# Two layers of a hybrid attention trunk in float32: neighbourhood heads scored in pairs, shared output weights, a fourth load buffer

## The chip, the cores and the metric

One core of one Trainium2 chip runs the whole program. The metric is the device time of one execution in microseconds. The kernel before took 1832.28 us (median of three runs, 1830.18 to 1832.47).

## The reference, cut to what matters

There are 256 latent tokens and 256 context tokens of 1024 features, and two layers with the same weights for both groups of tokens. Each layer is a half-step SwiGLU, then a mixing step, then a second half-step SwiGLU; every sub-layer is normalised on both sides and shifted, scaled and gated by a product with `w_ada`.

```python
def swiglu(h, w1, w2):
    a, b = jnp.split(h @ w1, 2, axis=-1)
    return (jax.nn.silu(a) * b) @ w2
...
    a_lat = neighbourhood_attention(aq, ak, av, akc, avc, rpb)      # 4 heads of 64
    b_lat = pool_mix(pin, pool_w, pool_scale)
...
    c_lat = diff_attention(q1, q2, k1 + k1c, k2 + k2c, v + vc, lam) # 4 heads, two softmaxes each
    y_lat = jnp.concatenate([a_lat, b_lat, c_lat], axis=-1) @ w_out
    if not with_ctx_out:      # the last layer
        return y_lat, None
    a_ctx = dense_attention(aqc, akc, avc)
    b_ctx = pool_mix(pinc, pool_w, pool_scale)
    c_ctx = diff_attention(q1c, q2c, k1c, k2c, vc, lam)
    y_ctx = jnp.concatenate([a_ctx, b_ctx, c_ctx], axis=-1) @ w_out
```

Latent queries see 512 keys (256 latent and 256 context), context queries see the 256 context keys. Layer zero gives both groups of tokens, layer one the latent group alone.

## The kernel before, in words

**Products.** Every float32 product is three products of split operands: an operand is held as a high part (rounded to fp32r) and a low part (the rest), and `mm` (L89) is called for high*high, high*low and low*high. One line (L90) thus records nearly all of TensorE's work. Transposes are recorded where they stand (L482, L536, L802).

**Weights.** A `Unit` (L165) is a weight tile of 512 KB. `load` (L177) brings it into one of three raw buffers (L117) over the queue of SyncE; `parts` splits it: ScalarE writes the high part (L186), VectorE the low part (L191), into a slot of `WS` (three slots), `XS` (five) or `MX` (five). `XS` and `MX` lie in the big tile `R`, which in the mixing step holds `MIXH`, `MIXL`, `PT`, `VAL` and `QK` instead. Units that VectorE reads straight from the raw buffer (`w_ada`, in `ada_v`, L448) are not split; each is read by four multiply-adds (L466).

**Order.** The order is written out by a planner. Work is cut into `Step`s (L206) with an assumed duration, steps that it must follow and delays behind them; `schedule` (L217) places main steps (matrix products) and side steps (attention, norms) on one clock, and `run` (L258) goes through the placed steps, issues the next load as soon as a raw buffer was split or read in that order, and the next split when its slot was given up in that order. A unit whose `after` names a mark is split only behind the step with that mark. Loads and splits go in the order of first use: a unit that can't be split holds up the splits behind it. Each engine works through its instructions in order.

**Modulation.** The products with `w_ada` run on VectorE beside the matrix products of three SwiGLU stages (`take`, L1287, deals out 6, 5 and 5 pieces). A piece's half has four steps of multiply-adds, then `red` (L470: four small products on TensorE sum over partitions, ScalarE copies the sums to `ROWB`, L474), then at once `fin` (L476: two transposes on TensorE, L482, for a shift or scale; for a gate, additions on VectorE into `GROW`, L439). A gate's half begins with `gate_rows` (L428), which loads two rows of constants into `GROW` over SyncE's queue.

**Mixing** (`mixing`, L717). Main steps compute queries and keys of six pairs of heads; side steps are the items. An item of a neighbourhood head (`na_attn`, L954) is one head and 128 queries: three products of 64 features (`scores`, L769) into one of two PSUM banks (`BS`), bias, maximum, exponential with its sum, reciprocal, scaling (L793 to L966), then transposes (`transpose_p`, L799) and the product with the values (`pv`). An item of a differential head (`diff_attn`, L1011) is 128 queries and both softmaxes: `scores2` (L779) issues six products in turn from partitions 0 to 63 and 64 to 127 into both banks. Context items are the same with 256 keys.

**Output product.** `wout_rows` (L1049) multiplies the mixed features by `w_out`, feature block by feature block; in layer zero it is called for the latent and then for the context group, and each call makes its own eight units, which go through the three `WS` slots. Then `tok_end` (L512) normalises and adds, and `pre_pair` (L528) transposes for the next SwiGLU.

## Time and profile before

| | |
|---|---|
| median of three runs | 1832.28 us |
| profiled execution, own time | 1824.12 us |
| its span, first to last instruction | 1822.3 us |
| mean granted TensorE clock | 0.987 |
| instructions | 24374 |
| moved from HBM | 257.51 MB |

A stretch A:B below is in microseconds from the span's start. By the trace the stages are: start to 68; first SwiGLU of layer zero to 400; mixing of layer zero from 455 to 660; its second SwiGLU to 1015 or so; layer one's first SwiGLU to 1400; mixing of layer one from 1456 to 1606; last SwiGLU from 1626. The ends of matrix products are modelled in a profile, so that a TensorE that is always "busy" need not be at its peak; the number of products in a stretch says more.

### The profile page before, as it was taken

How to read it: one execution, taken by the hardware profiler on the slowest of the kernel's cores; microseconds unless marked ns; L12 is line 12 of the kernel's file. 1: busy time of each engine (PE TensorE's matmuls, PEld its weight loads, DVE VectorE, ACT ScalarE, POOL GpSimd, SP SyncE). 2: the span in 40 equal slices, each digit the busy share in tenths (PEclk: the TensorE clock that was granted, in tenths of full speed). 3: DMA queues.
4: the chain of work that ended last, by engine and by line, in shares of the span. 5: the costliest groups of instructions: out<-in, count | busy, mean ns of one | idle time of the engine just before them, and what ended most of it. 6: DMA issues, size and time to landing. Idle time of an engine off the chain costs nothing.

```text
span 1822.3 us, 24374 instructions
## 1 busy us (share of the span) xinstructions
PE 1750.3 (96%) x9496; PEld 1452.9 (80%) x9496; DVE 1170.7 (64%) x1889; ACT 714.8 (39%) x1244; POOL 72.8 (4%) x128
## 2 busy tenths in 40 slices
PE   4999999999999999999999999999999999969998
PEld 3788777778977779878878798888887897859997
DVE  4756776667367875757758565666765737865553
ACT  3323222235267763323222442322223526654442
POOL 0000000001000400000000000000000100200000
PEclk8999999999999999999999999999999999979999
DMA  7836555554211152656545334645554431255662
GB/s 230 243 116 192 176 173 157 167 171 125 57 47 47 64 171 71 188 163 182 176 148 176 124 105 127 197 122 183 176 161 156 115 69 58 93 151 187 187 187 76
DMA packets 301187, 260.19 MB, mean 143 GB/s; under 512 B 18064, under 2 KB 246160, under 8 KB 301072
## 3 DMA queue, kind: packets, MB, share of 16 engines
q1 hardware_dynamic: 297216, 257.67, 46.5%
q8 instruction: 74, 1.21, 0.3%
q10 hardware_dynamic: 3856, 0.97, 0.2%
q14 instruction: 41, 0.34, 0.1%
HBM read 257.51 MB, written 1.10 MB: 142 GB/s over the span
## 4 chain that ended last, share of the span: by engine, by line
PE 65%; DMA 14%; DVE 12%; ACT 5%; issue 3%; POOL 1%; SPq 0%; ACTq 0%; DVEq 0%; POOLq 0%
PE bank L90 62%; DMA raw<-in_ffn_w_dram 10%; DVE sx L466 3%; DVE R L191 2%; ACT R L186 2%; DVE w L191 2%; DMA raw<-in_w_ada_dram 2%; ACT w L186 1%; DMA gtb<-in_w_ada_dram 1%; POOL sr L507 1%; PE bank L802 1%; PE bank L536 1%; DMA csrc<-in_c_dram 1%; DVE sx L464 0%; DVE X L524 0%
## 5 line engine op out<-in xcount | busy, mean ns | idle before, releaser
L90 PE MATMUL bank<-HH,R 128*128 128x512 f32 (+1 forms) x2028 | 531.7, 347 | 4.7 <-ACT R L186 2.5
L90 PE MATMUL bank<-HH,w 128*128 128x512 f32 (+1 forms) x1540 | 433.9, 359 | 0.4 <-DVE w L191 0.4
L90 PEld LDWEIGHTS bank<-HH,R 128*128 128x128 f32 x2028 | 356.3, 191 | 59.5 <-issue 7.2
L90 PE MATMUL bank<-R 128*128 128x512 f32 (+3 forms) x1632 | 364.1, 376 | 2.9 <-DVE YB L642 1.1
L90 PE MATMUL bank<-HL,R 128*128 128x512 f32 (+1 forms) x1014 | 349.5, 345 | 0.0
L90 PEld LDWEIGHTS bank<-R 128*128 128x128 f32 (+1 forms) x1632 | 278.5, 188 | 74.0 <-issue 9.7
L191 DVE TENSOR_TENSOR R<-raw,R 128x1024 fp32r<-128x1024 f32 (+1 forms) x177 | 214.7, 1216 | 173.5 <-ACT R L186 170.1
L466 DVE SCALAR_TENSOR_TENSOR sx<-raw,sc,sx 128x512 f32<-128x512 f32 x448 | 310.8, 745 | 21.8 <-DMA raw<-in_w_ada_dram 21.4
L186 ACT CAST R<-raw 128x1024 fp32r<-128x1024 f32 (+1 forms) x177 | 184.3, 1043 | 343.3 <-DMA raw<-in_ffn_w_dram 270.3
L90 PEld LDWEIGHTS bank<-HH,w 128*128 128x128 f32 x1540 | 274.1, 190 | 50.2 <-issue 12.0
L191 DVE TENSOR_TENSOR w<-raw,w 128x1024 fp32r<-128x1024 f32 (+1 forms) x153 | 187.5, 1226 | 161.8 <-ACT w L186 161.5
L90 PE MATMUL bank<-HL,w 128*128 128x512 f32 (+1 forms) x770 | 274.7, 357 | 0.0
L186 ACT CAST w<-raw 128x1024 fp32r<-128x1024 f32 (+1 forms) x153 | 159.9, 1046 | 279.8 <-DMA raw<-in_ffn_w_dram 199.6
L90 PE MATMUL bank<-w,R 128*128 128x512 f32 x960 | 236.0, 396 | 2.6 <-ACT R L1008 1.8
L90 PEld LDWEIGHTS bank<-w,R 128*128 128x128 f32 x960 | 178.1, 189 | 43.4 <-ACT R L1008 2.3
L90 PEld LDWEIGHTS bank<-HL,R 128*128 128x128 f32 x1014 | 193.3, 191 | 22.4 <-DVE HL L541 0.2
L90 PEld LDWEIGHTS bank<-HL,w 128*128 128x128 f32 x770 | 146.5, 190 | 20.6 <-issue 2.3
L591 DVE TENSOR_TENSOR sil<-sil,bank 128x512 f32<-128x512 f32 (+1 forms) x96 | 55.5, 578 | 77.9 <-PE bank L90 77.7
L593 ACT CAST R<-sil 128x512 fp32r<-128x512 f32 (+1 forms) x96 | 51.2, 533 | 135.0 <-DVE sil L591 135.0
L507 POOL TENSOR_TENSOR sr<-sr,eps 128x1 f32<-128x1 f32 x42 | 28.3, 674 | 1463.5 <-DVE sr L506 1444.5
L590 ACT ACTIVATE sil<-bank 128x512 f32<-128x512 f32 (+1 forms) x96 | 48.9, 510 | 90.7 <-PE bank L90 84.4
L360 DVE TENSOR_TENSOR R<-bank,R 128x512 fp32r<-128x512 f32 (+2 forms) x86 | 47.9, 561 | 33.8 <-ACT R L359 33.5
(145 smaller groups left out, 1211.8 us busy)
## 6 DMA issues: line engine op xcount, KB each, us to landing
raw<-in_ffn_w_dram SPq DMA_DIRECT2D x258, 512.0 KB
raw<-in_w_ada_dram SPq DMA_DIRECT2D x130, 512.0 KB
raw<-in_w_in_dram SPq DMA_DIRECT2D x40, 512.0 KB
raw<-in_w_out_dram SPq DMA_DIRECT2D x24, 512.0 KB
gtb<-in_w_ada_dram SPq DMA_DIRECT2D x10, 512.0 KB
gtb<-gate SPq DMA_DIRECT2D x10, 512.0 KB
raw<-in_ffn_w_dram SPq DMA_DIRECT2D x8, 384.0 KB
sx<-in_w_ada_dram SPq DMA_DIRECT2D x4, 512.0 KB
```

Of the source, the lines that this page charges most:

```text
L90: return nc.tensor.matmul(out=o, lhsT=l, rhs=r, start=start, stop=stop)
L186: ins = S.copy(out=self.hi, in_=self.raw)
L191: ins = self.lo_eng.tensor_tensor(out=self.lo, in0=self.raw, in1=self.hi.bitcast(F32), op=ALU.subtract)
L360: V.tensor_tensor(out=lo, in0=src, in1=hi.bitcast(F32), op=ALU.subtract)
L466: V.scalar_tensor_tensor(out=ACC[v], in0=u.raw[:, z, :], scalar=sv, in1=ACC[v], op0=ALU.mult, op1=ALU.add)
L507: G.tensor_tensor(out=a, in0=a, in1=mhalf, op=ALU.pow)
L536: nc.tensor.transpose(out=pt[:, z, t * P : (t + 1) * P], in_=y[:, t, k * P : (k + 1) * P], identity=ident)
L590: S.activation(out=sl[:, cs], in_=oa, func=AF.Silu)
L591: V.tensor_tensor(out=sl[:, cs], in0=sl[:, cs], in1=ob, op=ALU.mult)
L593: tab["hs"] = S.copy(out=uh[:, cs], in_=sl[:, cs])
L802: nc.tensor.transpose(out=b[:, n * P : (n + 1) * P], in_=e[:, n * P : (n + 1) * P], identity=ident)
```

## The change

- There are four raw buffers in place of three; a scratch tile is halved, and the statistics that wrote to it write to another tile. The ninth hidden slot moves to the end of `R`, so that each of the five `XS` slots covers exactly one tile of the mixing step: `PT`, three `VAL`, two `QK`.
- Neighbourhood heads are scored as differential heads were: both heads of a pair and 128 queries in one step, six products in turn into both banks, then both softmaxes, then two transposes as steps of their own.
- For the context group a step holds two heads (or both softmaxes) and all 256 queries: twelve products, each bank holding two blocks of 256 keys; maxima, reciprocals and transposes cover both blocks.
- `w_out` has eight units in each layer, used by both groups in layer zero. The first three go to `WS`, the others to `XS` slots behind marks: the mixing tile there must have had its last reader.
- `fin` is dealt out two side steps later than `red`, and `gate_rows` two steps later than before.

```diff
-    raws = [tile(f"raw{i}", [1024]) for i in range(3)]
+    raws = [tile(f"raw{i}", [1024]) for i in range(4)]
...
-    JUNK = tile("junk", [D], mybir.dt.bfloat16)
+    JUNK = tile("junk", [T], mybir.dt.bfloat16)
...
-    ST = Ring([tile(f"st{i}", [4]) for i in range(8)])
+    ST = Ring([tile(f"st{i}", [8]) for i in range(8)])
...
-    U_HI = [R[:, i * 1024 : i * 1024 + T] for i in range(NU)]
-    U_LO = [R[:, i * 1024 + T : (i + 1) * 1024] for i in range(NU)]
-    XS = [R[:, 9216 + i * 2048 : 9216 + (i + 1) * 2048].rearrange("p (a n) -> p a n", a=2) for i in range(5)]
+
+    U_AT = [i * 1024 for i in range(8)] + [19456]
+    U_HI = [R[:, i : i + T] for i in U_AT]
+    U_LO = [R[:, i + T : i + 1024] for i in U_AT]
+    XS = [R[:, 8192 + i * 2048 : 8192 + (i + 1) * 2048].rearrange("p (a n) -> p a n", a=2) for i in range(5)]
...
-                if j % 3 == 2:
-                    st.append(Step(lambda l=l, j=j, h=h: gate_rows(l, j, h)))
                 for q in range(4):
+                    if q == 2 and j % 3 == 2:
+                        st.append(Step(lambda l=l, j=j, h=h: gate_rows(l, j, h)))
...
+                st[-1].fin = True
...
+        def scores(q, k, g, qts):
+
+
+            o = [BS() for _ in range(2)]
+            nk = T // len(qts)
+            for n, qt in enumerate(qts):
+                q0 = GROUPS[g].start + qt * P
+                for i, (a, b) in enumerate(((0, 0), (1, 0), (0, 1))):
+                    for j in range(2):
+                        rs = slice(HD * j, HD * j + HD)
+
+                        mm(o[j][:, n * nk : (n + 1) * nk], q[rs, a, q0 : q0 + P], k[rs, b, :nk], i == 0 and n == 0, i == 2 and n == len(qts) - 1)
             return o
...
+        def softmax_exp(os_, es, n):
...
+            for j, o in enumerate(os_):
+                V.reduce_max(out=st[:, j * n : (j + 1) * n], in_=o.rearrange("p (a k) -> p a k", a=n), axis=AX.X, negate=True)
+                for a in range(n):
+                    c_, z = slice(a * T // n, (a + 1) * T // n), j * n + a
+                    behind(S.activation(out=es[j][:, c_], in_=o[:, c_], func=AF.Exp, bias=st[:, z : z + 1], accum_out=st[:, 4 + z : 5 + z]), table())
+            V.reciprocal(out=st[:, 0 : 2 * n], in_=st[:, 4 : 4 + 2 * n])
+            return st
+        def transpose_p(e, qts):
...
+            for i, qt in enumerate(qts):
+                for n in range(nk // P):
+                    nc.tensor.transpose(out=bv[:, n, i * P : (i + 1) * P], in_=e[:, i * nk + n * P : i * nk + (n + 1) * P], identity=ident)
+            split_ps(PT[:, 0, : nk // P, qs], PT[:, 1, : nk // P, qs], bv)
...
+        user = {}
+
+        def softmax_step(box, fn, tiles):
+
+            a = Step(fn, dur=1.0, after=[box["ready"]], needs=[user[z] for z in tiles if z in user])
             if items:
-                a.after.append((items[-1][0], (KN['ia'] * heads) * f + 0.3))
-            if len(items) >= ring:
-                a.needs.append(items[-ring][1])
-            b = Step(s2, dur=0.44 * f, after=[(a, KN['ib'] + (KN['ic'] + 0.8 * heads) * f)])
+                a.after.append((items[-1][0], KN["ia"] * 2 + 0.3))
+            return a
+        def turn_step(box, a, fn, tile_, more=0.0):
+
+            b = Step(fn, dur=0.44, after=[(a, KN["ib"] + KN["ic"] + 1.6 + more)])
...
-                def s1(hh_, qt, g=g, nk=nk, es=es):
-                    o = scores(box["q"], box["k"], HD * hh_, qt, g, nk)
+                po = {}
+
+                def s1(qts, tiles, g=g):
+                    os_ = scores(box["q"], box["k"], g, qts)
                     if g == LAT:
-                        ol = o[:, GROUPS[LAT]].rearrange("p (r c) -> p r c", r=ROWS)
-                        V.tensor_tensor(out=ol, in0=ol, in1=biases[hh_][:, 2 - 2 * qt : 2 - 2 * qt + ROWS, :], op=ALU.add)
-                    e, st = softmax_exp(o, nk, E)
-                    S.activation(out=e, in_=e, func=AF.Copy, scale=st[:, 2:3])
-                    es[hh_, qt] = e
-
-                def s2(hh_, qt, nk=nk, es=es):
-                    transpose_p(es[hh_, qt], nk, qt)
+                        for j, o in enumerate(os_):
+                            ol = o[:, GROUPS[LAT]].rearrange("p (r c) -> p r c", r=ROWS)
+                            V.tensor_tensor(out=ol, in0=ol, in1=biases[j][:, 2 - 2 * qts[0] : 2 - 2 * qts[0] + ROWS, :], op=ALU.add)
+                    n_ = len(qts)
+                    es = [E.t[z] for z in tiles]
+                    st = softmax_exp(os_, es, n_)
+                    for z in range(2 * n_):
+                        e = es[z // n_][:, (z % n_) * T // n_ : (z % n_ + 1) * T // n_]
+                        S.activation(out=e, in_=e, func=AF.Copy, scale=st[:, z : z + 1])
...
+                parts = [((0,), (0, 2)), ((1,), (1, 3))] if g == LAT else [((0, 1), (0, 1))]
...
+                def s1(qts, z, g=g):
+                    os_ = scores(box["q"], box["k"], g, qts)
+                    n_ = len(qts)
+                    es = [E.t[z], E.t[3]]
+                    st = softmax_exp(os_, es, n_)
+                    V.tensor_tensor(out=st[:, n_ : 2 * n_], in0=st[:, n_ : 2 * n_], in1=lam[l][:, 3:4].to_broadcast([P, n_]), op=ALU.mult)
+                    for a in range(n_):
+                        e1, e2 = [e[:, a * T // n_ : (a + 1) * T // n_] for e in es]
+                        S.activation(out=e1, in_=e1, func=AF.Copy, scale=st[:, a : a + 1])
+                        V.scalar_tensor_tensor(out=e1, in0=e2, scalar=st[:, n_ + a : n_ + a + 1], in1=e1, op0=ALU.mult, op1=ALU.add)
...
+                for qts in ((0,), (1,)) if g == LAT else ((0, 1),):
+                    z = e1s()
+                    a = softmax_step(box, lambda qts=qts, z=z, f=s1: f(qts, z), (z, 3))
+                    side += [a, turn_step(box, a, lambda z=z, qts=qts: transpose_p(E.t[z], qts), z)]
...
-            us = [Unit(w_out[l, k * P : (k + 1) * P, :], lo=lo_engine(KN['rowc'] if g == CTXG else KN['rowl'])) for k in ks]
...
+        wu = [Unit(w_out[l, k * P : (k + 1) * P, :]) for k in order]
+        ng = len(out_groups)
+        for name, z in (("nav", prods[: 4 * ng]), ("dv0", prods[: 6 * ng]), ("qk0", [it[0] for it in boxes[4]["items"]]),
+                        ("dv1", prods), ("pt", prods + [it[1] for it in items])):
+            side.append(Step(lambda: None, needs=list(z)))
+            side[-1].mark = f"{name}{l}"
+
+        for u, (sl, name) in zip(wu[3:], ((6, "nav"), (4, "dv0"), (7, "qk0"), (5, "dv1"), (3, "pt"))):
+            u.slots, u.after = (sl,), f"{name}{l}"
         for g in out_groups:
-            rows = wout_rows(g, order)
+            rows = wout_rows(g, order, wu)
...
-        o = []
+        o, late = [], []
         for _ in range(n):
-            o += f(*pieces.pop(0))
-        return o
+            for s in f(*pieces.pop(0)):
+                if s.fin:
+                    late = [s, 2]
+                    continue
+                o.append(s)
+                if late:
+                    late[1] -= 1
+                    if not late[1]:
+                        o.append(late[0])
+                        late = []
+        return o + late[:1]
```

## Rows read from the trace of the kernel before

**Rows 1.** The page: busy time, and the chain that ended last by engine

```profile
PE 1750.3 (96%) x9496; PEld 1452.9 (80%) x9496; DVE 1170.7 (64%) x1889; ACT 714.8 (39%) x1244; POOL 72.8 (4%) x128
...
PE 65%; DMA 14%; DVE 12%; ACT 5%; issue 3%; POOL 1%; SPq 0%; ACTq 0%; DVEq 0%; POOLq 0%
```

**Rows 2.** Busy time by stretch: us, engines busy (instructions), granted clock, DMA share, GB/s

```profile
112.00:360.00 248.00, 241.11 (x1090) 190.53 (x1088) 172.88 (x262) 61.79 (x84) 0.00 (x0) 0.99 0.55 170
210.00:260.00 50.00, 47.00 (x208) 37.37 (x212) 36.64 (x58) 14.00 (x18) 0.00 (x0) 0.97 0.58 179
500.00:620.00 120.00, 119.70 (x612) 89.39 (x611) 90.76 (x226) 86.89 (x225) 12.59 (x26) 1.00 0.15 46
620.00:730.00 110.00, 104.80 (x662) 92.01 (x662) 75.63 (x123) 59.55 (x118) 17.55 (x26) 1.00 0.37 115
730.00:914.00 184.00, 181.35 (x823) 145.75 (x821) 124.19 (x179) 54.75 (x71) 0.00 (x0) 0.99 0.58 180
1136.00:1400.00 264.00, 264.00 (x1211) 212.75 (x1210) 175.96 (x262) 76.57 (x98) 0.00 (x0) 1.00 0.53 162
1500.00:1600.00 100.00, 98.93 (x566) 79.66 (x565) 76.73 (x154) 69.66 (x147) 15.17 (x25) 1.00 0.27 84
1600.00:1626.00 26.00, 9.73 (x33) 6.47 (x31) 18.05 (x27) 14.38 (x29) 2.21 (x4) 0.65 0.63 185
```

**Rows 3.** Who waited for whom, TensorE: us in total, times, longest

```profile
PE bank L482 <- ACT rows L474: 5.3, 3, 2.6
...
PE bank L802 <- DVE R L360: 0.2, 1, 0.2
```

**Rows 4.** Timeline 229.9 to 236.5, three rows: start us, us, engine, line; idle before

```profile
234.99 1.04 ACT L186 CAST R<-raw 128x1024 fp32r<-128x1024 f32 x1 [3.82 <-DMA raw<-in_ffn_w_dram]
235.94 0.38 ACT L474 ACTIVATE rows<-bank 128x256 f32<-128x256 f32 x1
...
236.37 0.48 PE L482 MATMUL bank<-cst,rows 128*128 128x128 f32 x1 [2.63 <-ACT rows L474]
```

**Rows 5.** The DMA queue's waits: SP's own

```profile
SPq L432 <- DVE grow L439: 30.5, 8, 9.1
```

**Rows 6.** Timeline, TensorE, single scores of 256 and of 512 keys, and the next row

```profile
510.38 0.61 PE L90 MATMUL bank<-R 64*128 64x256 f32 x3
510.92 0.49 PE L90 MATMUL bank<-HL,w 128*128 128x512 f32 x1
...
515.38 0.96 PE L90 MATMUL bank<-R 64*128 64x512 f32 x3
516.27 0.50 PE L90 MATMUL bank<-HH,w 128*128 128x512 f32 x1
```

**Rows 7.** Timeline, TensorE, paired scores of 256 and of 512 keys, and the next row

```profile
535.03 0.62 PE L90 MATMUL bank<-R 64*128 64x256 f32 x6
535.58 0.74 PE L90 MATMUL bank<-HH,w 128*128 128x512 f32 x2
...
547.11 0.96 PE L90 MATMUL bank<-R 64*128 64x512 f32 x6
548.00 0.50 PE L90 MATMUL bank<-HH,w 128*128 128x512 f32 x1
```

**Rows 8.** Groups by form, 500 to 620 us: busy, mean ns | idle before

```profile
L795 ACT ACTIVATE YB<-bank,st 128x256 f32<-128x256 f32 x20 | 9.5, 475 | 3.7 <-DVE st L793 3.4 <-DVE YB L1025 0.2
...
L795 ACT ACTIVATION_READ_ACCUMULATOR YB<-bank,st 128x1 f32 x43 | 8.5, 198 | 0.0
...
L966 ACT ACTIVATE YB<-YB,st 128x256 f32<-128x256 f32 x8 | 3.9, 503 | 0.6 <-DVE st L796 0.5
```

**Rows 9.** The page: low parts of units, and the output weights' loads

```profile
L191 DVE TENSOR_TENSOR w<-raw,w 128x1024 fp32r<-128x1024 f32 (+1 forms) x153 | 187.5, 1226 | 161.8 <-ACT w L186 161.5
...
raw<-in_w_out_dram SPq DMA_DIRECT2D x24, 512.0 KB
```

**Rows 10.** Timeline, TensorE: a pair whose second bank came late

```profile
1577.90 1.63 PE L90 MATMUL bank<-R 64*128 64x512 f32 x6 [0.31 <-ACT YB L795]
```

More of the change, by code (lines that the diff above doesn't have):

```diff
@@ L210, in __init__ @@
             self.fn, self.units, self.dur, self.after, self.needs = fn, list(units), dur, list(after), list(needs)
-            self.low = low
+            self.low, self.fin = low, False
             self.t = None
@@ L556, in out_end @@
         for hf in range(2):
[L557 removed]
+            S.activation(out=JUNK, in_=o[hf], func=AF.Square, scale=RMS, accum_out=st[:, hf : hf + 1])
             V.tensor_tensor(out=gy[:, hf * T : (hf + 1) * T], in0=o[hf], in1=GTB[:, LAT, hf * T : (hf + 1) * T], op=ALU.mult)
@@ L790, in softmax_exp @@
-        def softmax_exp(o, nk, ring):
-            st = ST()
-            V.reduce_max(out=st[:, 0:1], in_=o, axis=AX.X, negate=True)
-            e = ring()[:, :nk]
-            behind(S.activation(out=e, in_=o, func=AF.Exp, bias=st[:, 0:1], accum_out=st[:, 1:2]), table())
-            V.reciprocal(out=st[:, 2:3], in_=st[:, 1:2])
-            return e, st
-        def transpose_p(e, nk, qt):
-            b = BT()
-            for n in range(nk // P):
-                nc.tensor.transpose(out=b[:, n * P : (n + 1) * P], in_=e[:, n * P : (n + 1) * P], identity=ident)
-            qs = slice(qt * P, (qt + 1) * P)
-            split_ps(PT[:, 0, : nk // P, qs], PT[:, 1, : nk // P, qs], b[:, :nk].rearrange("p (n q) -> p n q", q=P))
+        def scores(q, k, g, qts):
[7 more added lines that the diff above has]
+                        mm(o[j][:, n * nk : (n + 1) * nk], q[rs, a, q0 : q0 + P], k[rs, b, :nk], i == 0 and n == 0, i == 2 and n == len(qts) - 1)
+            return o
@@ L980, in s3 @@
                             split_ps(MIXH[rs, n, GROUPS[g]], MIXL[rs, n, GROUPS[g]], o[rs, z * SEQ : (z + 1) * SEQ])
-                for hh_ in range(2):
-                    for qt in range(2):
-                        st = item(box, lambda hh_=hh_, qt=qt, f=s1: f(hh_, qt), lambda hh_=hh_, qt=qt, f=s2: f(hh_, qt), nk, 1, 4)
-                        if g == LAT:
-                            st[0].after.append((bias_step, 1.5))
-                        side += st
+                parts = [((0,), (0, 2)), ((1,), (1, 3))] if g == LAT else [((0, 1), (0, 1))]
+                sm = []
+                for qts, tiles in parts:
+                    a = softmax_step(box, lambda qts=qts, tiles=tiles, f=s1: f(qts, tiles), tiles)
+                    if g == LAT:
+                        a.after.append((bias_step, 1.5))
+                    if sm:
+                        a.after.append((sm[-1], KN["ia"] * 2 + 0.3))
+                    sm.append(a)
+                    side.append(a)
+                for hh_ in range(2):
+                    for a, (qts, tiles) in zip(sm, parts):
+                        z = tiles[hh_]
+                        side.append(turn_step(box, a, lambda z=z, qts=qts: transpose_p(E.t[z], qts), z, 0.6 * hh_))
                     side.append(product(lambda hh_=hh_, f=s3: f(hh_), nk))
@@ L1036, in s3 @@
                     S.activation(out=RSTD[g], in_=o, func=AF.Square, scale=math.sqrt(D / P))
-                for qt in range(2):
-                    side += item(box, lambda qt=qt, f=s1: f(qt), lambda qt=qt, f=s2: f(qt), nk, 2, 3)
+                for qts in ((0,), (1,)) if g == LAT else ((0, 1),):
+                    z = e1s()
+                    a = softmax_step(box, lambda qts=qts, z=z, f=s1: f(qts, z), (z, 3))
+                    side += [a, turn_step(box, a, lambda z=z, qts=qts: transpose_p(E.t[z], qts), z)]
                 side.append(product(s3, nk))
@@ L1125, in mixing @@
                 at = diff_attn(n - 2, boxes[n])
-                if n == 2:
-                    at[0].needs += [it[1] for it in items[: -2 * len(out_groups)]]
                 side += ss + at
@@ L1185, in x_stat @@
         for t in range(2):
-            S.activation(out=JUNK, in_=xs[g][:, t], func=AF.Square, scale=RMS, accum_out=st[:, t : t + 1])
+            S.activation(out=S2T, in_=xs[g][:, t], func=AF.Square, scale=RMS, accum_out=st[:, t : t + 1])
         if g == LAT:
```

54 lines of the change are left out of this document (14 added, 40 removed).

## The prediction

> **What bounds the kernel now.** I read the page first. TensorE is busy for 96% of the span, and 65% of the chain that ended last is TensorE's; the rest of that chain is DMA (14%) and VectorE (12%) [rows 1]. So most of the time goes only if TensorE gets less to do, and a smaller part if it no longer waits.
>
> The table by stretch comes next, because a busy TensorE can still be slow. Three stretches are SwiGLU bodies with the same kinds of work: split weights and pieces of `w_ada`. In 1136 to 1400 TensorE starts 1211 products in 264 us, 0.2180 us each, with no idle time. In 112 to 360 it starts 1090 in 248 us, 0.2275 us each, and is idle for 6.9 us; in 730 to 914 it starts 823 in 184 us, 0.2236 us each [rows 2]. At the good stretch's pace the two would take 237.6 and 179.4 us. They lose 10.4 and 4.6 us, together 15.0.
>
> TensorE's waits say where. 5.3 us go to three waits of the transposes at L482 for ScalarE's copy at L474 [rows 3]. One of them shows the cause: the copy stands in ScalarE's queue behind the split of a unit whose load has not landed; the split has idled 3.82 us, the copy follows, and TensorE has idled 2.63 us [rows 4]. Around it the granted clock is 0.97 over 50 us: after the idle time a part ran at the lower of its two levels, 1.2 GHz in place of 2.4, and about 1.5 us more were lost [rows 2]. The loads are late because the raw buffers go round: 170 GB/s with three buffers of 0.524 MB means 9.3 us from one load of a buffer to its next [rows 2]. The queue of SyncE also stands still: 30.5 us in eight waits for `GROW` [rows 5].
>
> In mixing TensorE is the bound: it is busy for 119.70 of 120 us in 500 to 620, and for 98.93 of 100 us in 1500 to 1600; the end of layer one's mixing has 16.3 us without products in 1600 to 1626 [rows 2].
>
> **The change part by part.**
>
> *Scores.* A single score of 512 keys keeps TensorE for 0.89 us, from 515.38 to 516.27, and one of 256 keys for 0.54 us [rows 6]. A pair of six products takes the same 0.89 and 0.55 us: the two halves of the array run together [rows 7]. Latent neighbourhood scores: 4 heads, 2 blocks of queries, 2 layers are 16 singles, now 8 pairs; 8 x 0.89 = 7.1 us less. A context step of twelve products is not in the trace. Its bounds are one pair of 512 keys (the same number of columns, 0.89 us) and two pairs of 256 (1.10 us); it is nearest to the first, since nothing stands between its products. Neighbourhood context: 8 x 0.54 - 2 x 0.89 = 2.5 us less (2.1 at the other end). Differential context: 8 x 0.55 - 4 x 0.89 = 0.8 us less (0 at the other end). Together 10.4 us. Against it: a pair needs both banks, and where the second comes late it takes 1.63 instead of 0.96 us as the timeline shows it, 0.67 more [rows 10]. I count three such among 16 latent differential steps; at that rate 14 new steps give 14 x 3/16 x 0.67 = 1.8 us back. I take 8.5 us; the ends are 10.4 and, with every second bank late, 7.1 + 2.1 - 14 x 0.67, which is about nothing.
>
> VectorE and ScalarE do the same bias, maximum, exponential and scaling per key as before, and they cover for TensorE only while there are products between a step and its transposes. In 500 to 620 VectorE is busy for 90.76 us and ScalarE for 86.89 of 120 [rows 2], so a shorter stretch still has room: 112 us would hold both.
>
> Here a page speaks against the change. The Trainium skill, "TensorEngine Tiling (Array Packing)", section "Performance Considerations", says that tiling speeds up TensorE but not the emptying of PSUM, which may then be the bottleneck. By that the term would be nothing and the sum 16 us; by the busy times above it is 8.5 and the sum 24.5.
>
> *Fourth buffer and later `fin`.* At the good stretch's pace the first body needs 170 x 248 / 237.6 = 177 GB/s. Four buffers give 4 x 0.524 MB / 9.3 us = 225 GB/s if the round stays at 9.3 us, and enough up to a round of 11.8. With `fin` two side steps later the transposes find the copy done; queued behind TensorE's wait were all products of the body. `fin` takes its copies, additions and the gate's store with it, on VectorE's and ScalarE's queues, and nothing near needs them: the gates are loaded two thirds through a body. `gate_rows` and its four small loads move behind two weight loads on SyncE; it still waits for `GROW`, right behind the `fin` that reads it, but no longer for TensorE and ScalarE in front of that. If that wait stayed, it would hold up to 9.1 us of loads [rows 5], which is what the fourth buffer covers. The ends are 5.3 us (the transposes' waits alone) and 15.0 us (the good stretch's pace). I take 13, near the upper end, because 1136 to 1400 has the same work; the first loads of a body can still be late.
>
> *Shared output weights.* The 24 loads [rows 9] become 16. Eight splits go, with 8 x 1.23 us of VectorE [rows 9] and about as much of ScalarE (one such copy takes 1.04 us [rows 4]). None of this was TensorE's; what it frees is the wait in 620 to 730, where TensorE idles 5.2 us [rows 2] and the first units of the next SwiGLU queue behind those loads. I take 3 us of the 5.2; the other end is nothing. The new wait: the last two units can be split only behind the last product with the values, and the splits of the next SwiGLU queue behind them. That is 2 x (1.04 + 1.23) = 4.5 us, with three blocks of output rows (12 products each, at 0.22 us some 8 us) as cover. If the cover goes, 4.5 us in each layer are lost.
>
> *Costed at nothing:* the shifted slots (no two live tiles overlap), the halved scratch tile, the first 68 us, the merged maxima and reciprocals off the path, and the chain after the last head in layer one. For these I hold 3 us open in either direction.
>
> **Sum.** 8.5 + 13 + 3 = 24.5 us. The profiled execution took 1824.12 us by its own time and would take 1799.6. The median of the runs is 8.2 us above that execution, so I forecast 1832.28 - 24.5 = 1807.8 us; the forecast's own terms reach from 1800 to 1816.
>
> **The rivals.**
>
> A, *the loads stay late.* The round of a buffer lengthens to 11.8 us as more loads share the engines, and only the transposes' 5.3 us are won: 8.5 + 5.3 + 3 = 16.8, 1815.5 us. For it: the chain in the bodies alternates between loads and VectorE, which is busy for 172.88 of 248 us. Against: the DMA share is only 0.55 there [rows 2].
>
> B, *mixing becomes bound by the softmaxes* (the page's rule above): no gain from scores, 16 us, 1816.3 us. For it: both engines are at three quarters of 500 to 620. Against: TensorE hardly waited for a softmax so far, and its transposes at L802 waited 0.2 us in all [rows 3].
>
> C, *every wait goes*: 10.4 + 15.0 + 5.2 + 3 = 33.6 us, 1798.7 us.
>
> D, *slower: the joint steps end late and TensorE stands at the transposes.* The planner puts transposes 5.6 us behind a step (`turn_step`). A context step has four exponentials of 0.475 + 0.198 and four scalings of 0.503 us on ScalarE alone [rows 8], 4.7 us behind its first maximum. If a split or an evacuation gets in between, TensorE, which takes its queue in order, waits. With 14 joint steps this decides from 24.5 / 14 = 1.75 us each; at 2.5 us each it costs 35 us and the time is 1842.8. Against: differential heads have had two exponentials and the same 5.6 us, at 0.2 us of waits.
>
> E, *the pairs don't run together*: every second bank is late because other users of the two banks shift their turn; 14 x 0.67 = 9.4 us back instead of 1.8, so 16.9 us and 1815.4 us.
>
> **How the numbers follow.** Forecast 0.50, A 0.14, B 0.12, C 0.12, D 0.07, E 0.05. The prediction is the forecast's 1808. The range takes in A, B, C and E with what is held open on either side, and leaves out most of D: 1793 to 1822. Within 0.2% (3.7 us, about what a measurement can tell from no change) nothing but a sum of lower ends remains: 0.03; slower is D without its mild half, 0.05; faster 0.92.
>
> **What would show it.** Right: paired scores of 0.9 us in the neighbourhood part; no waits of L482; the two bodies at 0.219 us or less per product, with a granted clock of 1.00; sixteen loads of `w_out`; less than 3 us without products in 620 to 730's counterpart. Wrong: L802 with microseconds of waits (D, B), bodies still at 0.225 (A), or score steps of 1.5 us (E). A new idle stretch behind the last head of a layer would show the splits without cover.

## The result, and the profile after

The changed kernel takes 1799.97 us (median of 4 runs, 1797.86 to 1804.09) against 1832.12 us of the kernel before beside it (1830.18 to 1832.47): a ratio of 0.9829, 95% interval 0.9808 to 0.9851, or 32 us faster. In a later set on another chip the same two kernels stood at 1802.71 and 1830.46 us, 0.9854 (0.9834 to 0.9873), or 28 us. The forecast was 24.5 us and 1808 us; the range held the time.

The two profiled executions differ by 20.0 us only (1824.12 and 1804.09 us): of each kernel's four executions, the one of before was its fastest, the one of after its slowest. A second profile of each was therefore taken (the experiments `before_again` and `after_again`), and stretches are compared over both.

The page of the changed kernel, busy time by engine and the chain by engine; these answer to [rows 1]:

```profile
PE 1735.8 (96%) x9496; PEld 1447.9 (80%) x9496; DVE 1152.8 (64%) x1815; ACT 704.6 (39%) x1228; POOL 79.3 (4%) x128
...
PE 77%; DMA 8%; DVE 7%; ACT 4%; issue 2%; POOL 1%; ACTq 0%; DVEq 0%; POOLq 0%; SPq 0%
```

TensorE runs the same 9496 instructions in 14.5 us less busy time, and its share of the chain rises from 65 to 77%: DMA falls from 14 to 8% of it, VectorE from 12 to 7%.

Busy time by stretch of the changed kernel, the counterparts of [rows 2]; columns as there:

```profile
112.00:360.00 248.00, 243.92 (x1118) 195.02 (x1117) 181.81 (x274) 66.85 (x88) 0.00 (x0) 0.99 0.60 179
716.00:900.00 184.00, 183.19 (x838) 147.68 (x837) 125.20 (x182) 52.35 (x68) 0.00 (x0) 1.00 0.58 178
500.00:606.00 106.00, 105.15 (x562) 81.01 (x561) 81.76 (x166) 80.23 (x203) 14.66 (x24) 1.00 0.19 59
606.00:716.00 110.00, 106.19 (x676) 94.22 (x676) 66.05 (x112) 53.69 (x114) 16.86 (x26) 1.00 0.27 78
1116.00:1380.00 264.00, 264.00 (x1211) 212.67 (x1210) 172.82 (x259) 74.06 (x96) 0.00 (x0) 1.00 0.52 155
1490.00:1580.00 90.00, 89.35 (x505) 71.00 (x504) 71.83 (x132) 62.81 (x133) 18.45 (x22) 1.00 0.30 93
1580.00:1607.00 27.00, 11.47 (x48) 8.66 (x47) 17.55 (x28) 15.01 (x30) 2.22 (x4) 0.72 0.54 160
```

The second body comes to 184 / 838 = 0.2196 us per product (0.2236 before), the first only to 248 / 1118 = 0.2218 (0.2275 before; the good stretch has 0.2180). The figure of the second body depends on where the stretch is laid: in the second profile of before it is 0.2217 from 730 and 0.2236 from 734 us. Mixing is nearly as full of products as before.

Who waited for whom, the changed kernel: TensorE twice, and SyncE's queue for `GROW`; against [rows 3] and [rows 5]:

```profile
PE bank L538 <- DVE YB L528: 23.3, 8, 7.9
...
PE bank L807 <- DVE YB L1045: 0.8, 3, 0.3
```

```profile
SPq L180 <- DVE grow L440: 27.5, 10, 3.4
```

The waits of the old L482 (now L483) are gone. SyncE still waits 27.5 us for `GROW`, now in front of weight loads, but in steps of 3.4 us at most and not 9.1. Over all rows for `GROW` it waits 36.2 us, before 32.6: the wait was cut into shorter pieces and did not get less. The softmax transposes (L807) wait 1.3 us in all.

The transposes of the modulated activations (L538, `pre_pair`) stand at the start of each stage and serve as milestones. Their groups in the changed kernel: minimum, median and maximum in ns, first and last start in us:

```profile
L538 PE MATMUL bank<-cst,YB x32: 271/273/329, 412.5 to 445.3; 128*128 128x128 f32 x32
...
L538 PE MATMUL bank<-cst,YB x32: 271/273/331, 641.4 to 677.7; 128*128 128x128 f32 x32
...
L538 PE MATMUL bank<-cst,YB x32: 271/273/328, 1026.6 to 1056.9; 128*128 128x128 f32 x32
...
L538 PE MATMUL bank<-cst,YB x32: 271/273/477, 1404.8 to 1440.9; 128*128 128x128 f32 x32
...
L538 PE MATMUL bank<-cst,YB x16: 415/421/476, 1596.5 to 1607.6; 128*128 128x128 f32 x16
```

Differences of these starts give the length of every stage. The same milestones of all kernels run here make the table that the rest rests on (us; "front" is from the first to the last transposes ahead of a mixing, "heads" from there to the first ahead of the next SwiGLU, "w_out 0" from there to the last; a body runs to the next first start):

| kernel | first body | front 0 | heads 0 | w_out 0 | second body | third body | front 1 | heads 1 | to the end |
|---|---|---|---|---|---|---|---|---|---|
| before | 418.1 | 34.7 | 203.1 | 40.1 | 350.1 | 377.8 | 31.8 | 159.9 | 206.7 |
| before_again | 420.8 | 34.9 | 203.1 | 41.3 | 352.0 | 378.5 | 33.1 | 160.4 | 206.7 |
| after | 412.5 | 32.8 | 196.1 | 36.3 | 348.9 | 378.2 | 36.1 | 155.6 | 205.8 |
| after_again | 409.6 | 33.8 | 196.3 | 36.3 | 349.5 | 378.2 | 36.0 | 155.6 | 205.8 |
| p_raw4 | 406.1 | 32.9 | 203.5 | 41.3 | 352.5 | 378.5 | 33.2 | 157.5 | 206.6 |
| p_fin | 417.1 | 35.0 | 203.1 | 41.6 | 347.2 | 381.4 | 32.7 | 160.3 | 206.9 |
| p_pairs | 420.2 | 34.8 | 196.3 | 40.4 | 349.6 | 378.4 | 32.5 | 159.7 | 206.0 |
| p_wout | 417.7 | 34.8 | 202.1 | 36.0 | 350.9 | 378.1 | 31.9 | 157.0 | 206.0 |
| u_fin | 406.5 | 33.0 | 196.0 | 36.4 | 357.6 | 378.4 | 37.2 | 155.4 | 205.8 |
| f_pair | 408.1 | 33.7 | 194.0 | 36.3 | 350.1 | 377.7 | 36.5 | 155.3 | 205.4 |
| f_pair_again | 410.5 | 33.8 | 193.9 | 36.3 | 349.7 | 378.0 | 37.3 | 155.8 | 205.8 |
| f_front | 411.3 | 33.5 | 193.9 | 36.3 | 349.9 | 378.5 | 33.6 | 155.1 | 206.0 |
| f_mix | 406.3 | 33.5 | 193.8 | 36.3 | 349.4 | 378.1 | 33.7 | 157.0 | 205.6 |

The mean of the two profiles of after against that of before: first body -8.4, front 0 -1.5, heads 0 -6.9, w_out 0 -4.4, second body -1.9, third 0, **front 1 +3.6**, heads 1 -4.6, the end -0.9. One stage got longer. Together they make 24.9 us: by the two pairs of profiles the gain is smaller than by the medians.

Two of these boundaries do not part the same work in every kernel. Before, then after, w_out 0 and front 1:

```profile
655.90:696.00 40.10, 36.92 (x232) 32.35 (x232) 33.74 (x51) 26.75 (x51) 4.32 (x6) 1.00 0.58 171
1423.90:1455.70 31.80, 29.23 (x188) 26.09 (x187) 25.15 (x38) 19.09 (x37) 5.22 (x7) 1.00 0.47 130
```

```profile
641.40:677.70 36.30, 33.98 (x207) 29.46 (x208) 28.62 (x46) 21.32 (x44) 4.35 (x6) 1.00 0.41 117
1404.80:1440.90 36.10, 32.78 (x212) 30.05 (x211) 27.77 (x42) 21.25 (x40) 5.51 (x7) 0.97 0.55 134
```

In w_out 0 TensorE starts 25 products fewer, which went to the second body; in front 1 it starts 24 more, which came out of the heads. Sums over both sides of a boundary can be compared: w_out 0 and second body 390.2 and 393.3 us before, 385.2 and 385.8 after; front 1 and heads 1 191.7 and 193.5 before, 191.7 and 191.6 after.

The scores, in TensorE's timeline of the changed kernel: a neighbourhood pair, a differential step that came apart, and the last joint context step, each with the row behind it:

```profile
486.08 0.97 PE L90 MATMUL bank<-R 64*128 64x512 f32 x6
486.98 0.50 PE L90 MATMUL bank<-HH,w 128*128 128x512 f32 x1
...
1538.69 0.96 PE L90 MATMUL bank<-R 64*128 64x512 f32 x3
1539.58 0.38 PE L90 MATMUL bank<-HH,w 128*128 128x256 f32 x1
...
1541.17 0.96 PE L90 MATMUL bank<-R 64*128 64x512 f32 x3
1542.06 0.39 PE L90 MATMUL bank<-HH,w 128*128 128x256 f32 x1
...
607.97 1.19 PE L90 MATMUL bank<-R 64*128 64x256 f32 x12
609.09 0.70 PE L90 MATMUL bank<-sx,YB 128*128 128x256 f32 x2
```

The pair keeps TensorE for 0.90 us, as forecast; the differential step takes twice 0.89 us, because its two heads run one after the other; the twelve products of the context step take 1.12 us. The context steps of differential heads in before, which [rows 7] was to show, ran as two threes as well; one of the eight:

```profile
578.12 0.62 PE L90 MATMUL bank<-R 64*128 64x256 f32 x3
...
580.24 0.61 PE L90 MATMUL bank<-R 64*128 64x256 f32 x3
```

### The profile page after: what moved, and what is told of

The parts are those of the page before. It is cut to its first block, busy times and chain, and to the rows that moved or that the text cites. A ratio compares the mean times of both kernels' runs of the same rounds, so it can differ in the third digit from the quotient of the medians.

```text
span 1802.3 us, 24258 instructions
## 1 busy us (share of the span) xinstructions
PE 1735.8 (96%) x9496; PEld 1447.9 (80%) x9496; DVE 1152.8 (64%) x1815; ACT 704.6 (39%) x1228; POOL 79.3 (4%) x128
## 4 chain that ended last, share of the span: by engine, by line
PE 77%; DMA 8%; DVE 7%; ACT 4%; issue 2%; POOL 1%; ACTq 0%; DVEq 0%; POOLq 0%; SPq 0%
PE bank L90 75%; DMA raw<-in_ffn_w_dram 5%; DVE w L192 1%; DVE R L192 1%; ACT w L187 1%; ACT R L187 1%; DMA gtb<-in_w_ada_dram 1%; PE bank L538 1%; PE bank L807 1%; POOL sr L509 1%; DVE sx L467 1%; DMA raw<-in_w_in_dram 1%; DMA csrc<-in_c_dram 1%; DVE X L526 0%; DVE YB L528 0%
## 5 line engine op out<-in xcount | busy, mean ns | idle before, releaser
L90 PE MATMUL bank<-HH,R 128*128 128x512 f32 (+1 forms) x2012 | 524.7, 346 | 0.0
L90 PEld LDWEIGHTS bank<-HH,R 128*128 128x128 f32 x2012 | 351.8, 189 | 51.9 <-issue 7.2
L90 PE MATMUL bank<-R 128*128 128x512 f32 (+3 forms) x1728 | 381.7, 378 | 5.0 <-ACT YB L642 2.3
L90 PEld LDWEIGHTS bank<-R 128*128 128x128 f32 (+1 forms) x1728 | 293.4, 188 | 75.3 <-issue 6.4
L192 DVE TENSOR_TENSOR R<-raw,R 128x1024 fp32r<-128x1024 f32 (+1 forms) x182 | 220.9, 1219 | 163.9 <-ACT R L187 162.4
L187 ACT CAST R<-raw 128x1024 fp32r<-128x1024 f32 (+1 forms) x182 | 189.3, 1045 | 312.9 <-DMA raw<-in_ffn_w_dram 208.6
L192 DVE TENSOR_TENSOR w<-raw,w 128x1024 fp32r<-128x1024 f32 (+1 forms) x140 | 171.6, 1226 | 157.6 <-ACT w L187 156.4
L187 ACT CAST w<-raw 128x1024 fp32r<-128x1024 f32 (+1 forms) x140 | 146.3, 1046 | 244.4 <-DMA raw<-in_ffn_w_dram 161.4
L90 PE MATMUL bank<-w,R 128*128 128x512 f32 x864 | 209.7, 394 | 3.7 <-DVE YB L644 1.8
L90 PEld LDWEIGHTS bank<-w,R 128*128 128x128 f32 x864 | 159.7, 188 | 42.6 <-issue 3.2
```

Of the source, the lines that this page charges most:

```text
L90: return nc.tensor.matmul(out=o, lhsT=l, rhs=r, start=start, stop=stop)
L187: ins = S.copy(out=self.hi, in_=self.raw)
L192: ins = self.lo_eng.tensor_tensor(out=self.lo, in0=self.raw, in1=self.hi.bitcast(F32), op=ALU.subtract)
```

## The experiments

**The four parts, each alone on the kernel before**, on one chip, against 18 runs of before (median 1830.08 us).

*p_raw4.*

```diff
-    raws = [tile(f"raw{i}", [1024]) for i in range(3)]
+    raws = [tile(f"raw{i}", [1024]) for i in range(4)]
-    JUNK = tile("junk", [D], mybir.dt.bfloat16)
+    JUNK = tile("junk", [T], mybir.dt.bfloat16)
```

> The kernel before with the fourth load buffer alone (and the scratch tile halved to make room). Theory 1, the loads were late because three buffers go round too slowly: both bodies come to 0.219 us per product or less, the three waits of the transposes for the copy of the modulation rows fall below 1 us, and the time falls by 10 to 15 us (ratio 0.992 to 0.9945). Rival, SyncE's queue stands behind the gate rows whatever the number of buffers: the 30 us of SyncE's waits stay, the bodies stay above 0.222 us per product, and no more than 5 us are won (ratio 0.997 to 1.000).

Measured: 1815.05 us, 0.9918 (0.9901 to 0.9934), 15.0 us faster. By stretch, the two bodies, and SyncE's wait:

```profile
112.00:360.00 248.00, 246.56 (x1139) 197.65 (x1137) 186.14 (x282) 70.22 (x91) 0.00 (x0) 1.00 0.60 183
718.00:902.00 184.00, 179.57 (x821) 144.21 (x819) 121.96 (x180) 51.28 (x67) 0.00 (x0) 1.00 0.56 172
```

```profile
SPq L432 <- DVE grow L439: 69.4, 9, 22.8
```

The first body comes to 248 / 1139 = 0.2177 us, better than the good stretch, and ends 12 to 15 us earlier. The second stays at 184 / 821 = 0.2241 us. So theory 1 holds in one body and the rival in the other: SyncE now stands 69.4 us for `GROW`, 36 of them in the first body, where nothing comes late for it, and 29 in the second.

*p_fin.*

```diff
-                if j % 3 == 2:
-                    st.append(Step(lambda l=l, j=j, h=h: gate_rows(l, j, h)))
                 for q in range(4):
+                    if q == 2 and j % 3 == 2:
+                        st.append(Step(lambda l=l, j=j, h=h: gate_rows(l, j, h)))
...
+                if s.fin:
+                    late = [s, 2]
+                    continue
```

> The kernel before with the later closing step of the modulation pieces and the later gate rows alone, three buffers. Theory 1: the transposes' waits (10.9 us in three waits) go, but the loads stay late, so 3 to 6 us are won (ratio 0.997 to 0.998) and the first body stays above 0.222 us per product. Rival a, the waits only move to the next user of a late load: 0 to 2 us (ratio 0.999 to 1.000). Rival b, SyncE's standing queue was the cause of the late loads: 10 us or more (ratio below 0.995) with three buffers only.

Measured: 1826.23 us, 0.9977 (0.9964 to 0.9990), 4 us faster. The two bodies:

```profile
112.00:360.00 248.00, 243.73 (x1114) 192.64 (x1113) 177.46 (x265) 66.09 (x87) 0.00 (x0) 0.99 0.57 172
731.00:915.00 184.00, 182.35 (x833) 146.58 (x832) 125.20 (x183) 53.49 (x69) 0.00 (x0) 1.00 0.58 178
```

As theory 1 has it: 0.2226 us per product in the first body, and 0.2209 in the second, which is where its gain lies (347.2 against 350.1 and 352.0 us). The expectation gave the waits of the transposes as 10.9 us; they are 5.3 in three waits [rows 3], and 4 us came of them. Its third body takes 381.4 us, where every other kernel has 377.7 to 378.5; no run here shows why.

*p_pairs.* The hunks of `scores`, `softmax_exp`, `transpose_p`, `na_attn` and `diff_attn` of the change, on the old slots.

> The kernel before with the paired scores and joint context steps alone. Theory 1: TensorE's time in score steps falls by 8 to 9 us, nearly all in layer 0, and the time with it: 7 to 9 us won (ratio 0.995 to 0.996). Rival a, the end of each mixing is bound by the w_out loads and splits, which come no earlier: 0 to 4 us (ratio 0.998 to 1.000). Rival b, fewer and longer steps also leave the other engines freer: 12 us or more (ratio below 0.9935).

Measured: 1820.61 us, 0.9946 (0.9930 to 0.9963), 9.5 us faster: slightly more than theory 1. The heads of layer zero take 196.3 us in place of 203.1; those of layer one 159.7, as before. TensorE's time in the score steps falls by 6.7 us, less than theory 1 has it, and all of it in layer zero; the other 3 us can be put down to no stage.

*p_wout.* The hunks with `wu`, its marks and the shifted slots.

```diff
-            us = [Unit(w_out[l, k * P : (k + 1) * P, :], lo=lo_engine(...)) for k in ks]
+        wu = [Unit(w_out[l, k * P : (k + 1) * P, :]) for k in order]
+        for u, (sl, name) in zip(wu[3:], ((6, "nav"), (4, "dv0"), (7, "qk0"), (5, "dv1"), (3, "pt"))):
+            u.slots, u.after = (sl,), f"{name}{l}"
```

> The kernel before with the output weights of layer one shared by the two groups alone (and the slots shifted for it). Theory 1: 8 loads and 8 splits fewer free the end of layer zero's mixing: 2 to 5 us (ratio 0.997 to 0.999). Rival a, the last two units can be split only behind the last products, so the gain there is lost again behind the last head: 0 or slower (ratio 1.000 to 1.003). Rival b, the end of the mixing and the start of the next body both gain: over 6 us (ratio below 0.9965).

Measured: 1823.14 us, 0.9959 (0.9943 to 0.9974), 7 us faster; its profiled run was its fastest of seven, 1816.32. More than theory 1, and rival b's figure. By milestones some 3 us lie in the stage of the output weights of layer zero and the body behind it (386.9 together for 390.2; the stage alone falls from 40.1 to 36.0, but with some 25 products fewer), and 3 us where I expected nothing, in front and heads of layer one (188.9 for 191.7), in which the weights serve one group only. There the change gives the units slots of their own too. SyncE's queue, in the timeline of before and then of this kernel, the last six loads of `w_out`:

```profile
1558.72 29.77 SPq L179 DMA_DIRECT2D raw<-in_w_out_dram  x6
```

```profile
1553.26 22.87 SPq L181 DMA_DIRECT2D raw<-in_w_out_dram  x6
```

They go out over 23 us in place of 30. That this is what shortens the stage is likely, but it was not tried by itself; with the fourth buffer alone the stage has 157.5 us too.

The four gains add up to 15.0 + 3.9 + 9.5 + 6.9 = 35.3 us; the changed kernel won 28 to 32. Some 3 to 8 us are lost when the parts meet.

**Second profiles, and two edits of the changed kernel**, on one chip.

> The kernel before, unchanged, for a second profile of it. Its first profiled execution took 1824.1 us by its own time, while its other runs took 1830 to 1832. Theory 1: the runs differ where loads are late, so a profile near 1830 us has the first SwiGLU body (112 to 360 us) and the other weight stretches slower, and the mixing stretches the same to within 1 us. Rival: the runs differ by the granted clock alone, evenly over the span.

Measured: 1832.59 us by the profiled execution. Against the first profile, 8.5 us longer in span: first body +2.7, w_out 0 +1.2, second body +1.9, third +0.7, front 1 +1.3, the rest together +0.7. Theory 1: the stages with many loads differ and heads 0 does not (203.1 both times). That the time of a run of before depends on when its loads land fits this, but is not shown.

> The changed kernel, unchanged, as the measure for the two kernels beside it and for a second profile. Expected: a ratio of 0.981 to 0.985 again, and a profile in which the first body ends earlier than the 412.5 us of the first profile (the first profiled execution was the slowest of its four).

Measured: 1802.71 us, 0.9854 (0.9834 to 0.9873), just outside what I expected; the first body ends at 409.6 us, as expected.

*u_fin*, the p_fin hunks undone in the changed kernel:

> The changed kernel with the closing steps of the modulation pieces and the gate rows back in their old places, four buffers kept. Theory 1, the fourth buffer alone makes the loads punctual, so the old place costs nothing more: within 2 us of the changed kernel run beside it. Rival a, the later place is worth with four buffers what it was worth with three (4.2 us): 3 to 5 us slower than the changed kernel. Rival b, it now holds the work of a later step up: 3 to 6 us faster, with the first body ending near 406 us as with the fourth buffer alone.

Measured: 1808.10 us, 0.9882 (0.9864 to 0.9900), 5.4 us slower than the changed kernel: rival a, and just above its bound. But its stages show two effects. The first body ends 3 us earlier (406.5), as rival b has it; the second takes 8 us more (357.6 for 349.5). TensorE, 690 to 1030 us:

```profile
PE bank L483 <- ACT rows L475: 3.3, 2, 1.8
PE bank L90 <- DVE YB L643: 3.2, 1, 3.2
```

```profile
690.00:1030.00 340.00, 332.00 (x1569) 269.47 (x1568) 214.54 (x314) 97.31 (x137) 2.19 (x4) 0.99 0.52 158
```

The changed kernel, in its second profile, has 338.12 us busy with 1625 products in the same stretch. SyncE stands 29 us for `GROW` there, at most 13.5, as with the fourth buffer alone. So with four buffers the later place is worth 8 us in the second body. That the buffer itself helps there, no run shows: with the old place p_raw4 stands at 352.5 us, no better than before, and u_fin at 357.6 against the 350.9 of p_wout, which has three buffers and the same number of products in that body. `fin` and `gate_rows` went back together, so their shares are not parted.

*f_pair.*

```diff
-                    for j in range(2):
+                    for j in (1, 0):
...
-                        mm(o[j]...)
+                        ins = mm(o[j]...)
+                        if n == 0 and i == 0:
+                            if j == 1:
+                                first = ins
+                            else:
+                                behind(ins, first)
```

> The changed kernel with each score pair kept together: the two heads' first products change places, and the first head's may not be ordered ahead of the second's, so none starts before both banks are free. In the changed kernel about half of the differential steps still run as two separate threes of 0.89 us. Theory 1: TensorE's time in scores falls by another 8 to 14 us, and the time by 5 to 12 us against the changed kernel run beside it. Rival a: the pair now waits for the second bank with nothing else to do, the softmaxes end later, and TensorE's idle time grows by what the pairs save: within 2 us. Rival b: slower by 3 us or more, with waits of the transposes behind the scalings.

Measured: 1798.93 us, 0.9830 (0.9811 to 0.9849), 3.8 us faster than the changed kernel, between theory 1 and rival a. The differential step shown above, in its timeline:

```profile
1535.12 0.97 PE L90 MATMUL bank<-R 64*128 64x512 f32 x6
1536.02 0.50 PE L90 MATMUL bank<-HH,w 128*128 128x256 f32 x2
```

Adding the score steps over the timeline (first product to the next other row): before 29.4 us in layer zero and 15.9 in layer one, after 23.7 and 16.0, here 21.0 and 12.0. The 2.7 us in layer zero shorten its heads by 2.3; the 3.9 us in layer one shorten nothing (155.3 for 155.6): TensorE is busy for 142.1 us of that stage in place of 145.5, so what the pairs save there comes back as idle time, as rival a has it. Two differential steps of layer zero still run as two threes (from 568.29 and from 576.50).

**The longer front of layer one.** In the timeline of `after_again`, SyncE's queue, then ScalarE, then TensorE:

```profile
1416.75 1.34 SPq L824 DMA_DIRECT2D YB<-in_na_rpb_dram  x2
1420.69 0.37 SPq L180 DMA_DIRECT2D raw<-in_w_in_dram  x1
1421.16 2.68 SPq L824 DMA_DIRECT2D YB<-in_na_rpb_dram  x2
...
1427.32 1.05 ACT L187 CAST R<-raw 128x1024 fp32r<-128x1024 f32 x1 [2.72 <-DMA raw<-in_w_in_dram]
1428.28 0.62 ACT L521 ACTIVATE junk<-YB 128x512 bf16<-128x512 f32 x1
...
1435.82 0.44 PE L538 MATMUL bank<-cst,YB 128*128 128x128 f32 x2 [3.17 <-DVE YB L528]
```

The loads of the attention bias go out around a weight load of the front; ScalarE's split idles 2.72 us for its load, the square that the context group's chain needs stands behind it, and TensorE idles 3.17 us for that chain (2.5 us in before). In the issue order of the kernels with the fourth buffer alone, or the shared weights alone, the bias stands behind all of the front's loads; with both parts it passes the last two.

*f_pair_again, f_front, f_mix*, on one chip (before: 1832.03 us).

> The changed kernel with each score pair kept together, unchanged from the run before, as the measure for the two kernels beside it. Expected: a ratio of 0.981 to 0.985 again, and the front of layer one's mixing (from the end of the first SwiGLU to the last modulated transposes) as long as in the changed kernel, 36 us.

Measured: 1802.27 us, 0.9841 (0.9824 to 0.9859); front 1 is 37.3 us. That is 3.3 us above its first set, so its gain over the changed kernel (3.8 us side by side) is about as large as what two sets differ by.

*f_front.*

```diff
         def after_front(ins):
 
-            return behind(ins, early[-1].dma)
+            for u in early:
+                behind(ins, u.dma)
+            return ins
```

> The pairs kept together, and the bias and pooling loads ordered behind all eight weight loads of the mixing's front and not behind the last of them alone. In the changed kernel four to six of these small loads pass the seventh weight load on SyncE's queue; ScalarE's split of that weight waits 1.9 and 2.7 us for its load, the squares of the other group's chain stand behind it, and TensorE waits 2.4 and 3.2 us for the chain. Theory 1: both waits fall below 1 us, the front of layer one's mixing comes back from 36 to 32 or 33 us, and 3 to 6 us are won against the kernel beside it. Rival a: the chain is late for VectorE's splits ahead of it and not for the load; the waits stay, within 2 us. Rival b: the bias comes late now and the first scores wait for it, slower by 2 us or more.

Measured: 1797.07 us, 0.9813 (0.9795 to 0.9831), 5.2 us faster than the kernel beside it. SyncE's queue and TensorE's wait:

```profile
1412.91 7.85 SPq L180 DMA_DIRECT2D raw<-in_w_in_dram  x4
1420.86 2.05 SPq L831 DMA_DIRECT2D YB<-in_na_rpb_dram  x3
```

```profile
PE bank L538 <- DVE YB L528: 1.8, 1, 1.8
```

Front 1 falls from 37.3 to 33.6 us and TensorE's wait from 3.4 to 1.8: theory 1, although the wait does not go below 1 us. The wait is 1.6 of the 3.7 us; the other 2 are busy time for the same products at a higher granted clock, 1.00 for 0.92. f_pair_again, then f_front:

```profile
1402.20:1439.80 37.60, 34.19 (x214) 31.56 (x213) 28.00 (x43) 21.34 (x40) 5.50 (x7) 0.92 0.55 132
```

```profile
1403.40:1437.30 33.90, 32.15 (x215) 29.25 (x214) 25.18 (x38) 20.43 (x38) 5.51 (x7) 1.00 0.58 138
```

In layer zero the wait stays (1.9 us after 2.2) and the front is as long as before; there rival a is right, or another load is late.

*f_mix.*

> As the kernel with the bias loads behind the front's weights, and in the first SwiGLU body alone the closing steps of the modulation pieces and the gate rows back in their old places. With old places everywhere the first body ended 3 us earlier (406.5 against 409.6 us) and the second body took 8 us more (357.6 against 349.5). Theory 1: the two do not depend on each other, so 2 to 4 us are won against the kernel beside it. Rival: the 3 us are the spread between runs in the first body, within 1.5 us.

Measured: 1795.93 us, 0.9807 (0.9791 to 0.9824), 1.1 us faster by the medians, inside the rival's bound. The profile has the first body end at 406.3 us, at 0.2174 us per product:

```profile
112.00:360.00 248.00, 247.02 (x1141) 198.06 (x1140) 186.69 (x283) 70.30 (x91) 0.00 (x0) 1.00 0.60 183
```

All three profiles with four buffers and the old place in the first body (p_raw4, u_fin, f_mix) end it at 406 us, and the five with the later place at 408 to 413. But the profile of f_front was the slowest of its four runs (1799.87), and the times of the two kernels show 1.1 us, and f_mix takes 1.9 us longer in the heads of layer one; whether the 3 us come through is open. This version is the fastest one run, some 36 us below the kernel before; that it beats the changed kernel rests on two sets, 0.9807 against 0.9829 and 0.9854 on other chips.

## Why the prediction was right or wrong

The side and the range were right, and the forecast was 3 to 8 us short. Of its signs two were missed: the first body's pace (below), and TensorE is 3.8 us without products in 606 to 716, the counterpart of 620 to 730, where less than 3 were to show. By its steps:

**Scores, 8.5 us: near in size by luck, wrong in place.** Alone they gave 9.5 us (heads 0 and 1 together 7.0 in that profile), but the 8.5 were a sum of TensorE's time, and TensorE's time in score steps fell by 6.7 us there and by 5.6 in the changed kernel. By terms, TensorE's time over both layers in us, from the timelines of before and after (the 1.8 us held back were for late banks in the new steps):

| score steps | before | after | difference | forecast |
|---|---|---|---|---|
| latent, neighbourhood | 14.4 | 7.8 | -6.6 | -7.1 |
| context, neighbourhood | 3.6 | 3.1 | -0.5 | -2.5 |
| context, differential | 8.7 | 5.7 | -3.1 | -0.8 |
| latent, differential | 18.4 | 23.0 | +4.6 | 0 |
| held back | | | | +1.8 |

The six products at 535.03 in [rows 7], which I took for a differential context step, are two neighbourhood singles side by side; all eight differential context steps of before ran as two threes, 1.1 us each and not 0.55. Layer zero gave all of the gain. I had counted eight latent singles of layer one as gain too, 4 x 0.89 = 3.6 us. Three of its four neighbourhood pairs do take 0.9 us, but differential steps that ran as pairs before came apart: in the timeline of before four of layer one's eight are clean sixes, after it is one, and three are separate threes. That is rival E in seven of the sixteen latent differential steps of the two layers, with 0.89 us for the second three and not 0.67. Two of the sixteen ran so in before already (571.23 and 573.63, 611.80 and 615.10), and I had counted only late second banks. I had bounded a late second bank by a pause of the pair; the products of the first head may also be issued ahead, with other work between the heads. Of the six joint context steps one takes 0.91 us (at 543.91) and the others 1.1 to 1.8, three of them with other products in between and two with all twelve in a row (1.58 at 520.53, 1.12 at 607.97); the upper bound was too low.

Rival B's rule (the Trainium skill, "TensorEngine Tiling (Array Packing)", "Performance Considerations", which names it for a speedup of 4x) would have let nothing remain. A pair here halves TensorE's time: heads 0 fell by 6.8 us with TensorE busy for 105.15 of 106 us, so here the emptying of PSUM was no bound. In layer one's mixing, where the pairs kept together gave nothing, TensorE's idle time grew by what they saved; no run here shows what binds at its end.

**Fourth buffer and later `fin`, 13 us: the mechanism was right, the two parts were mixed up.** I gave the buffer the loads and `fin` the transposes, with ends of 5.3 and 15.0. Alone they gave 15.0 and 3.9 us. The forecast of 0.219 us per product was about met in the second body (0.2196, and 0.2188 in the second profile) and missed in the first (0.2216 to 0.2218, for 0.2177 with the buffer alone). The buffer's mechanism holds in the first body; in the second the gain goes with the later place (347.2 us in p_fin with three buffers), and the buffer's part is not shown. The step that failed is that `fin` takes its copies, additions and the gate's store with it "and nothing near needs them": in the first body the later place costs about 3 us by the milestones. TensorE waits there 2.3 us for ScalarE's copy at L642, a wait that none of the three kernels with four buffers and the old place shows in that body. That this wait is what the later place costs is likely, not shown. The remark on `gate_rows`, that its wait would hold loads if it stayed, was right in that the wait stayed (with the buffer alone it grew from 30.5 to 69.4 us); in the first body it cost nothing that shows.

**Shared output weights, 3 us: mis-sized.** They gave 7 alone; some 3 us in the stage where I saw 5.2 without products (620 to 730) and the body behind it, about as forecast, and 3 us in front and heads of layer one, for which I had nothing: I had costed the slots and marks at nothing. The new wait that I feared, the last two units' splits behind the last head, didn't show: TensorE is idle for 2.3 us in the stage behind the last head of layer zero (641.4 to 677.7), for 3.2 before.

**Costed at nothing, within 3 us: wrong in one place.** The front of layer one got 3.6 us longer. Part of that is the 24 products that moved into it, but ordering the small loads alone gave 3.7 us of it back with the same products (f_front). I moved "the shifted slots" off the path because no two live tiles overlap, and did not ask in what order SyncE's queue would then serve the loads.

**Sum.** Alone the parts gave 35 us, close to rival C's 33.6; together 28 to 32; front 1 (3.7 us by f_front) and the first body (about 3 by u_fin) are where runs show some given back. The forecast of 1808 stood on 8.2 us between the profiled execution and the median. In three sets before has 1830.1 to 1832.0 us, with single runs from 1823.6 to 1836.1, so that correction was right.

## What to carry to other kernels

Two edits that cure lateness are not a sum: the fourth buffer gave its gain in the first body, where the later place then cost some 3 us; in the second body the gain needed the later place, and the buffer with the old place stood 8 us longer. Where small loads could pass large ones, 3.7 us of a stage were lost. When a part frees buffers or slots, read the issue order of the DMA queue at each stage's start, for loads that pass the one on which the chain depends, and order them behind all of those loads, not behind the last in the program. Instructions that only pay when they run side by side must be tied to each other; else one half can go ahead, with other work in between, and a pair costs two (1.78 us for 0.89 here). A stage between two milestones need not hold the same work in two kernels: count its instructions before its time is compared.

## What the runs showed that was not expected

- SyncE standing still for up to 22.8 us in the first body, behind four buffers, cost nothing that shows: that body had a better pace than the good stretch (0.2177 us per product for 0.2180, clock 1.00). In the second body of u_fin, with waits of up to 13.5 us, the stage took 8 us more than with the later place.
- Six score products of 64 rows by 512 columns cost 0.89 us when both heads' are adjacent, and 1.78 us when they are issued as two threes; tying them together took 6.6 us off TensorE's score steps, but no more than 3.8 us off the time.
- Runs of one unchanged kernel differ by 8.5 us in span, nearly all of it in the stages with many weight loads and none in the heads of layer zero.
